# A hybrid decoder block: the state-space parameters' load, the pace of the state-space preparation, the transposes' banks and the place of the taps' matrices

## The chip, the cores and the metric

The kernel runs on one core of a Trainium2 chip. The metric is device time in microseconds (us), the median of three runs. Besides, one execution was recorded by the hardware profiler; the profile and the trace are of that one. Engines are named as in the profile: PE is TensorE, PEld its weight loads, DVE is VectorE, ACT is ScalarE, POOL is GpSimd, SP is SyncE. Each engine takes its own instructions in order and waits for others through semaphores.

## The reference

A decoder block over 528 positions (16 learned ones and 512 of the sequence), width 2048, float32. From one RMS-normalised input two branches are computed, latent attention with 16 heads and a diagonal complex state-space layer; both are gated, added, projected, and followed by a SwiGLU feed-forward part and a last norm.

```
n = rms_norm(h, norm_mix)
q_lat, kv_lat, k_r, u, gates = split(n @ w_in)
q, kv = rms_norm(q_lat) @ w_q_up, rms_norm(kv_lat) @ w_kv_up      # 16 heads
attn_out = mla_attention(q_nope, rope(q_rope), k_nope, rope(k_r), v) @ w_attn_proj
# state space: 64 groups, 64 states, 16 channels each
step = exp(log_step); ab = exp(lam * step); bb = (ab - 1) / lam * b
x[t] = ab * x[t-1] + bb @ u[t];  y[t] = Re(c @ x[t]) + d * u[t]
ssm_out = (gelu(y) @ w_glu_val) * sigmoid(gelu(y) @ w_glu_gate)
mixed = sigmoid(g0) * attn_out + sigmoid(g1) * ssm_out
h = h + mixed @ w_out
h = h + (silu(m @ w_ffn_gate) * (m @ w_ffn_up)) @ w_ffn_down,  m = rms_norm(h, norm_ffn)
out = rms_norm(h, norm_final)[16:]
```

## The kernel before

**Products.** Float32 products are made of three reduced ones: each operand is split into a high half (ACT rounds it, L262) and a low half (VectorE subtracts, L263), and TensorE adds high x high, high x low and low x high. Weights come as a stream of blocks of 128 x 1024 on SP's queue. `st.use()` hands out the next block and emits the splits of the blocks up to two ahead; the halves lie in rings of three.

**Order before the attention.** `dense` (L390) makes one output tile of 128 rows: sixteen weight tiles, two blocks, in banks of PSUM. PSUM has eight banks: psA and psB two each, psD two together, psQ and psV one each. The tiles are eight of u (the state-space input), four of q, four of kv, and one for the rotated key. u and kv tiles and the rope tile take psA and psB together, q tiles psA alone. When a tile is done VectorE evacuates it, for q and kv ACT squares it, and GpSimd or VectorE adds the squares.

**What runs beside.** After each block `dense` calls `bg()` (L364). It first runs what was put off to this turn (norms and pieces of norms), then it takes work from a generator. The generator says with each `yield` how much VectorE time it has just emitted, and each turn has an allowance of 5.0. Its work is emitted in program order into all engines, between the blocks. What is left after the rope tile is emitted at once by `run_out` (L935).

**The generator** is `ssm_first` (L663). `ssm_params` (L519) computes from 96 values a partition the powers of the discretised state matrix: exponentials, sine and cosine as polynomials on VectorE, then tables by doubling. Then, for each of four groups of 16 state-space groups:

- loads of b and d; copies on ACT into C48 (L709) and the first columns of the rotation table ER (L714), then two doublings of ER on VectorE (L717);
- `expand` twice (L724, L726), each of two halves of three VectorE products of 128 x 1024: the input matrix BL into ssA and the output matrix into ER;
- `taps` (L672): 64 small matmuls into psD, the response of the layer to one input over eight positions;
- `transposed` (L680): BL is turned by TensorE, four 128 x 128 transposes to a bank of psB, and evicted by ACT (L684) into BT, a tile in ssB; four such banks a group, then BT goes to DRAM;
- one group later `toeplitz` (L686): VectorE adds the direct term to the taps, eight DMAs store them (L690), GpSimd clears a tile of 128 x 2048 in ssB (L692), eight DMAs read the taps back shifted (L695), so that the tile holds a block-triangular matrix of taps for each of 16 state-space groups, and a DMA stores the tile (L697).

The matrices are read again only after the attention, by `load_t` in `ssm_main`. All these DMAs are issued by GpSimd, as are the stores of u (L874, eight a tile), the rope tables' load for the key (L938) and the DMA that moves half of the rotated key to other partitions (L943).

**The attention.** `run_out` is followed by the key's rope, then by a loop of turns, `for i in range(-1, HEADS + 1)`. In a turn the entries of `TURN` (L1173) are emitted for three heads: the scores of head i, transposes and value product of head i - 1, and key, query and value projections of head i + 1. GpSimd has in it: the loads of rotated queries `load_qs` into QS (L1005), a memset in every second turn (L1069), and after every fourth head two additions of `up_rope`, on which ACT then waits. The outputs of the heads are kept in `raw`, sixteen half tiles which lie in ssA, ssB, T1, T2, v and w; before, all are allocated ahead of the loop.

The sum of squares for a norm, `rstd_of` (L414), is made by a matmul with ones into psQ, and for 528 columns into psQ and psV.

Of the kernel before, what the change touches and what calls it, by code (L numbers as in the profile page):

```python
# [22 lines left out]
F32 = mybir.dt.float32  # L23
# [7 lines left out]
P = 128  # L31
# [3 lines left out]
SEQ = 512  # L35
# [11 lines left out]
CL = 8  # L47
NC_ = T // CL
BP = 8
BG = 16  # L50
# [247 lines left out]
def _emit(nc, sp, pp, dp, A, out):  # L298
# [3 lines left out]
    def sb(shape, dt, tag, bufs=1):  # L302
        cnt[0] += 1
        return sp.tile(shape, dt, tag=tag, name=f"{tag}_{cnt[0]}", bufs=bufs)
# [3 lines left out]
    def ps(shape, tag):  # L308
        cnt[0] += 1
        return pp.tile(shape, F32, tag=tag, name=f"ps{tag}_{cnt[0]}", bufs=BANKS[tag])  # L310
# [137 lines left out]
    POOL.dma_start(identb, A["identb"])  # L448
    mask = sb([P, P], BF, "mask")
    POOL.dma_start(mask, A["mask"])  # L450

    acc = sb([P, T], F32, "acc")
    rstd_x = sb([P, T], F32, "rstd")
# [63 lines left out]
             v(T1), v(T2))  # L517

    def ssm_params():  # L519
        prm = sb([P, 3, 32], F32, "sprm")  # L520
        POOL.dma_start(prm, A["sprm"])
        lr, li, ls = prm[:, 0], prm[:, 1], prm[:, 2]
        w = sb([P, 16, 32], F32, "sw")
        wi = sb([P, 32], I32, "swi")
# [16 lines left out]

        step, rr, th = w[:, 0], w[:, 1], w[:, 2:4]
        exp_(step, ls)
        yield 6
        tt(rr, lr, step, MUL)
        exp_(rr, rr)
        yield 6
        tt(w[:, 2], li, step, MUL)
        ts(w[:, 3], w[:, 2], 8.0, None, MUL)
        q, a, z = w[:, 4:6], w[:, 6:8], w[:, 8:10]  # L550
# [7 lines left out]
        ts(z, z, -MAGIC, None, ADD)  # L558
        stt(q, z, -4.0, q, MUL, ADD)
        tt(z, a, a, MUL)  # L560
        yield 3
        ts(sn, z, 1.0 / 362880, None, MUL)
        for c in (-1.0 / 5040, 1.0 / 120, -1.0 / 6):
            stt(sn, sn, c, z, ADD, MUL)
# [7 lines left out]
        ts(tA, tA, -1.0, 2.0, MUL, ADD)  # L572
        tt(q, q, tA, MUL)
        cs_, sn_ = w[:, 6:8], w[:, 2:4]
        yield 5
        tt(tA, sn, z, MUL)
        tt(sn_, co, q, MUL)
        tt(sn_, sn_, tA, ADD)
# [8 lines left out]
        tt(pw[:, 1, :, 1], rr, sn_[:, 0], MUL)  # L587
        t1 = w[:, 8:12].rearrange("p a b -> p (a b)")
        t2 = w[:, 12:16].rearrange("p a b -> p (a b)")
        yield 5  # L590
        for m in (1, 2, 4):
            bc = lambda i: pw[:, i, :, m:m + 1].to_broadcast([P, 32, m])
            v1 = t1[:, :32 * m].rearrange("p (a b) -> p a b", b=m)
# [3 lines left out]
        tt(e8[:, 2], rr, rr, MUL)  # L597
        tt(e8[:, 2], e8[:, 2], e8[:, 2], MUL)
        tt(e8[:, 2], e8[:, 2], e8[:, 2], MUL)
        yield 5  # L600
        nr, den, s1 = w[:, 8], w[:, 9], w[:, 10]
        ab_re, ab_im = pw[:, 0, :, 1], pw[:, 1, :, 1]
        ts(nr, ab_re, -1.0, None, ADD)
# [9 lines left out]
        tt(s1, nr, li, MUL)  # L613
        tt(cf[:, 1], cf[:, 1], s1, SUB)
        tt(cf[:, 1], cf[:, 1], den, MUL)
        yield 4

        T1 = sb([P, 2 * T], F32, "T1")
        T2 = sb([P, 2 * T], F32, "T2")
# [43 lines left out]
    def ssm_first():  # L663
# [14 lines left out]
            return pk  # L678

        def transposed(b, BL, BT, j):  # L680
            pt = ps([P, 4, P], "B")
            for i in range(4):
                PE.transpose(pt[:, i], BL[:, i % 2, j + i // 2], ident)
            ACT.activation(BT[:, j:j + 2].rearrange("p a b c -> p (a b) c"), pt, AF.Copy)  # L684

        def toeplitz(b, pk, Dg):  # L686
            g0 = b * BG
            tt(Dg, pk[:, :BG * 16], Dg, ADD)
            for i in range(CL):
                POOL.dma_start(kd[:, g0:g0 + BG, i], Dg[i * 16:(i + 1) * 16].rearrange("p (g o) -> p g o", o=16))  # L690
            TT = sb([P, BG, P], F32, "ssB")
            POOL.memset(TT, 0.0)  # L692
            for i in range(CL):
                s = CL - 1 - i
                POOL.dma_start(TT[i * 16:(i + 1) * 16, :, s * 16:],  # L695
                               kd[:, g0:g0 + BG, 0:i + 1].rearrange("p g t o -> p g (t o)"))
            POOL.dma_start(wt[b], TT.rearrange("p g m -> p (g m)"))  # L697

        behind = None
        for b in range(4):  # L700
# [17 lines left out]
                yield 1.0 + 0.05 * k  # L718
            POOL.dma_start(ed[b], ER.rearrange("p a j c -> p a (j c)"))
            if behind:  # L720
                toeplitz(*behind)
                yield 0.4
            BL = sb([P, 2, BP, CL * 16], F32, "ssA")
            yield from expand(BL, Bt, js, 0, 1, T1, T2)  # L724
# [11 lines left out]
            POOL.dma_start(bd[b], BT.rearrange("p j a c -> p (j a c)"))  # L736
            yield 0.1
        yield 5
        toeplitz(*behind)

    def ssm_main():

# [137 lines left out]
    for j in range(8):  # L880
        if j == 2:
            d2 = ps([P, 2, 512], "D")
            o = [(d2[:, 0, :HT], 0, HT), (d2[:, 1, :HT], HT, T)]
        else:
            o = halves("A", "B")
        dense(n, KT, o)
        pend.append((j, o))
        if j >= 2:
            while pend:
                evac_u(*pend.pop(0))  # L890
        if j == 2:
            beside(ssm_first(), 5.0)


    def normed(raw, acc_, nn, gcol, tag0, per):
# [48 lines left out]


    raw = {}
    for tag, h0, c in (("ssA", 0, 4), ("ssB", 4, 4), ("T1", 8, 2), ("T2", 10, 2), ("v", 12, 2), ("w", 14, 2)):
        t = sb([P, c, SEQ], F32, tag)
        for i in range(c):
            raw[h0 + i] = t[:, i]  # L950
    QS = sb([P, 2, SEQ], R, "U")
    pt01 = sb([P, 2, 4, P], R, "S10")
    pt23a = sb([P, 2, 4, P], R, "S11")
# [184 lines left out]
    def pv(h, pair):  # L1138
        if pair == 0:
            pvt[h] = ps([P, 512], "V")  # L1140
        o = pvt[h][:, pair * 256:(pair + 1) * 256]
        tm, ta = vt[h // 2]

        c = slice((h % 2) * P, (h % 2) * P + P)
        fl = lambda t, x, a: t[:, x, a:a + 2].rearrange("p a b -> p (a b)")
        mm(o, tm[:, c], ptm[:, 2 * pair:2 * pair + 2].rearrange("p a b -> p (a b)"), True, False)
        items = []
        srcs = [(1, pt01, 2), (2, pt01, 0)] if pair == 0 else \  # L1150
            [(1, pt23a, 0), (2, pt23a, 2), (3, pt23b, 2), (4, pt23b, 0)]
        for kb, t, a in srcs:
            v_ = ta[(kb - 1) // 2]
            items.append((v_[:, (kb - 1) % 2, 0, c], v_[:, (kb - 1) % 2, 1, c], fl(t, 0, a), fl(t, 1, a)))
        for n_, (vh, vl, ph, pl) in enumerate(items):
            mm(o, vh, ph, False, False)
            mm(o, vh, pl, False, False)
            mm(o, vl, ph, False, n_ == len(items) - 1)
        if pair == 1:
            ACT.activation(raw[h], pvt.pop(h), AF.Copy)  # L1160

    def rest():
# [32 lines left out]
    for i in range(-1, HEADS + 1):  # L1195
        norm_prev()
        for who, what in TURN:
            head = i + {"c": -1, "s": 0, "u": 1}[who]
            if 0 <= head < HEADS:
                what(head)  # L1200


    H2 = SEQ // 2
# [623 lines left out]
```

## Time and profile before

| | |
|---|---|
| median of three runs | 2838.66 us (2837.74 to 2839.67) |
| profiled execution | 2837.2 us, its span 2835.4 us |
| mean granted clock of TensorE | 0.986 |
| PE busy | 2747.7 us, 97% of the span |
| VectorE busy | 2049.9 us, 72% |
| ACT busy | 1222.6 us, 43% |
| GpSimd busy | 496.1 us, 17% |

Times in the trace are counted from the span's start. An instruction's row has its start, its length, engine, line of the kernel, operation, what it writes and reads, and in brackets how long the engine had stood idle before it and what ended that. DMA issues on GpSimd are shown with the time the engine took to issue them, not with the transfer. The granted clock is a share of full speed, and a mean under 1 in a stretch says that TensorE ran part of it slower. Blocks of DMA rows name the tile and its source (`ssB<-kd`: into a tile in ssB, from the taps in DRAM).

### The profile page before, as it was taken

To read this page: it belongs to the slowest core of one execution; us is meant where nothing else is said; L and a number is where in the kernel's file an instruction comes from. 1 tells how busy PE (TensorE), PEld (TensorE's weight loads), DVE (VectorE), ACT (ScalarE), POOL (GpSimd) and SP (SyncE) were. 2 spreads that over 40 slices of the span, in tenths; PEclk is the share of its full clock that TensorE was granted. 3 is DMA by queue.
4 is the path that set the end of the run, shared out by engine and by line. 5 is a ranking of instruction groups with operands and counts; after the bars stand their busy time and mean duration, and the time that the engine had idled before them with its cause. 6 is when DMAs were issued, how large, how long until landed. Compare 5 with 4: busy or idle time off the path is not lost.

```text
span 2835.4 us, 50272 instructions
## 1 busy us (share of the span) xinstructions
PE 2747.7 (97%) x20782; PEld 2593.5 (91%) x20782; DVE 2049.9 (72%) x2682; ACT 1222.6 (43%) x1786; POOL 496.1 (17%) x768
## 2 busy tenths in 40 slices
PE   8977899999999999999999999999999999999997
PEld 8867799977899999888889999999999999999997
DVE  6876566666367777433468888888888888788896
ACT  4223455542354445322234444444444445353445
POOL 3344211113221201112112000000000003030102
PEclk9988899999999999999999999999999999999998
DMA  5465222259664434444443343334333337474542
GB/s 173 127 193 159 92 68 68 68 201 352 213 231 158 164 138 160 142 148 139 135 135 135 135 139 127 137 127 142 128 126 134 135 133 255 164 268 164 198 160 97
DMA packets 129204, 436.86 MB, mean 154 GB/s; under 512 B 18736, under 2 KB 23536, under 8 KB 126864
## 3 DMA queue, kind: packets, MB, share of 16 engines
q1 hardware_dynamic: 76672, 263.36, 27.1%
q0 software_dynamic: 51520, 169.19, 18.0%
q8 instruction: 163, 2.67, 0.4%
q10 hardware_dynamic: 784, 1.11, 0.1%
q14 instruction: 65, 0.53, 0.1%
HBM read 348.61 MB, written 81.40 MB: 152 GB/s over the span
## 4 chain that ended last, share of the span: by engine, by line
PE 81%; DVE 6%; DMA 3%; issue 2%; POOL 1%; ACT 1%; DVEq 0%; ACTq 0%; POOLq 0%
PE psA L316 48%; PE psB L316 20%; PE psQ L316 6%; PE psV L316 5%; PE psD L316 1%; DVE wlo L263 1%; DVE S L323 1%; DVE T L323 1%; DVE ev L323 1%; DMA U<-ud 0%; DMA ER<-td 0%; PE psA L1127 0%; DMA ssB<-kd 0%; DMA T<-td 0%; DVE cmb L243 0%
## 5 line engine op out<-in xcount | busy, mean ns | idle before, releaser
L316 PE MATMUL psA<-S,whi 128*128 128x256 f32 (+2 forms) x5136 | 1124.1, 309 | 13.0 <-ACT whi L262 6.2
L316 PEld LDWEIGHTS psA<-S,whi 128*128 128x128 f32 x5136 | 845.6, 189 | 68.3 <-ACT whi L262 7.0
L316 PE MATMUL psA<-S,wlo 128*128 128x256 f32 (+2 forms) x2568 | 792.0, 308 | 8.9 <-DVE wlo L263 8.8
L263 DVE TENSOR_TENSOR wlo<-raw,whi 128x1024 fp32r<-128x1024 f32 (+1 forms) x479 | 591.8, 1236 | 184.6 <-ACT whi L262 182.5
L262 ACT ACTIVATE whi<-raw 128x1024 fp32r<-128x1024 f32 (+1 forms) x479 | 504.0, 1054 | 412.7 <-PE psA L316 182.5
L316 PEld LDWEIGHTS psA<-S,wlo 128*128 128x128 f32 x2568 | 485.5, 189 | 35.9 <-DVE wlo L263 10.4
L263 DVE TENSOR_TENSOR wlo<-cmb,whi 128x1024 fp32r<-128x1024 f32 x225 | 275.2, 1223 | 96.6 <-ACT whi L262 95.6
L316 PE MATMUL psB<-S,whi 128*128 128x256 f32 (+1 forms) x1632 | 331.2, 284 | 0.6 <-ACT ssB L684 0.5
L262 ACT ACTIVATE whi<-cmb 128x1024 fp32r<-128x1024 f32 x225 | 237.6, 1056 | 203.1 <-DVE wlo L263 138.9
L316 PEld LDWEIGHTS psB<-S,whi 128*128 128x128 f32 x1632 | 267.0, 191 | 1.4 <-ACT ssB L684 0.8
L316 PE MATMUL psB<-S,wlo 128*128 128x256 f32 (+1 forms) x816 | 231.0, 283 | 0.0
L316 PEld LDWEIGHTS psB<-S,wlo 128*128 128x128 f32 x816 | 155.0, 190 | 0.0
L1335 POOL DMA_DIRECT2D td<-sC x22 | 15.8, 717 | 764.6 <-ACT ev L1254 679.6
L316 PE MATMUL psA<-H,whi 128*128 128x512 f32 (+2 forms) x448 | 120.3, 356 | 15.1 <-DVE ev L323 11.3
L316 PEld LDWEIGHTS psA<-H,whi 128*128 128x128 f32 x448 | 78.1, 193 | 26.3 <-DVE ev L323 11.6
L243 DVE TENSOR_TENSOR cmb<-raw,raw 128x1024 f32<-128x1024 f32 x75 | 91.4, 1219 | 5.5 <-DMA raw<-in_wst 4.4
L323 DVE TENSOR_TENSOR H<-H,psA 128x256 f32<-128x256 f32 (+1 forms) x42 | 22.5, 536 | 97.2 <-POOL H L323 88.4
L243 DVE TENSOR_TENSOR cmb<-cmb,raw 128x1024 f32<-128x1024 f32 x75 | 91.5, 1220 | 0.0
L243 DVE TENSOR_TENSOR cmb<-raw,cmb 128x1024 f32<-128x1024 f32 x75 | 91.5, 1220 | 0.0
L243 DVE TENSOR_TENSOR raw<-raw,raw 128x1024 f32<-128x1024 f32 x75 | 91.4, 1219 | 0.0
L1254 ACT ACTIVATE ev<-psA 128x256 f32<-128x256 f32 x114 | 43.4, 381 | 100.6 <-PE psA L316 100.6
L316 PE MATMUL psA<-H,wlo 128*128 128x512 f32 (+2 forms) x224 | 78.2, 349 | 0.0
(680 smaller groups left out, 5464.7 us busy)
## 6 DMA issues: line engine op xcount, KB each, us to landing
raw<-in_wst SPq DMA_DIRECT2D x485, 512.0 KB, 3.7
td<-sC POOLq DMA_DIRECT2D x22, 512.0 KB, 3.2
td<-H POOLq DMA_DIRECT2D x40, 256.0 KB, 3.3
S<-td POOLq DMA_DIRECT2D x40, 256.0 KB, 6.9
H<-sg POOLq DMA_DIRECT2D x16, 512.0 KB, 3.9
cd<-ER POOLq DMA_DIRECT2D x8, 512.0 KB, 6.2
bd<-ssB POOLq DMA_DIRECT2D x4, 1024.0 KB, 4.8
wt<-ssB POOLq DMA_DIRECT2D x4, 1024.0 KB, 5.5
```

Source lines behind the costliest of these rows:

```text
L243: self.nc.vector.tensor_tensor(t, g(a), g(b), op=op)
L262: self.nc.scalar.activation(hi[:, a:b], w[:, a:b], AF.Copy)
L263: self.nc.vector.tensor_tensor(lo[:, a:b], w[:, a:b], hi[:, a:b], op=ALU.subtract)
L316: PE.matmul(o, lhsT=l, rhs=r, start=start, stop=stop, skip_group_check=more)
L323: eng.tensor_tensor(o, a, b, op=op)
L1254: ACT.activation(snap[name], o, AF.Copy)
L1335: POOL.dma_start(dst[0:2].rearrange("f p n -> p f n"), pair)
```

## The change

Five things are changed.

1. The 96 parameters a partition are loaded with the constants at the start, no longer at the generator's first step.
2. The amounts that `ssm_params` states with its yields are smaller, and the allowance of a turn is 4.7, no longer 5.0.
3. `transposed` writes into psQ and psV in turn, no longer into psB.
4. `toeplitz` is cut in two. In the generator `keep_taps` adds the direct term and stores the taps. The clearing, the shifted reads and the store are a new `toeplitz(b)` which the attention's loop calls at the end of its turns 0 to 4: turn i clears and reads the matrix of group i, in two tiles of half the size with eight reads each, and stores the two tiles of group i - 1. Groups 0 and 3 use ssB, group 1 T1 and T2, group 2 v and w.
5. The tiles of `raw` are allocated when the first head that lies in each is evicted.

```diff
@@ -448,6 +448,8 @@
     mask = sb([P, P], BF, "mask")
     POOL.dma_start(mask, A["mask"])
+    prm = sb([P, 3, 32], F32, "sprm")
+    POOL.dma_start(prm, A["sprm"])
@@ -517,8 +519,6 @@
     def ssm_params():
-        prm = sb([P, 3, 32], F32, "sprm")
-        POOL.dma_start(prm, A["sprm"])
...
         exp_(step, ls)
-        yield 6
+        yield 4.2
         tt(rr, lr, step, MUL)
         exp_(rr, rr)
-        yield 6
+        yield 4.4
...
-        yield 3
+        yield 2.4
...
-        yield 5
+        yield 3.6
...
-        yield 5
+        yield 2.4
...
-        yield 5
+        yield 4.4
...
-        yield 4
+        yield 3.2
@@ -678,23 +678,16 @@
         def transposed(b, BL, BT, j):
-            pt = ps([P, 4, P], "B")
+            pt = ps([P, 4, P], "QV"[j // 2 % 2])
...
-        def toeplitz(b, pk, Dg):
+        def keep_taps(b, pk, Dg):
             g0 = b * BG
             tt(Dg, pk[:, :BG * 16], Dg, ADD)
             for i in range(CL):
                 POOL.dma_start(kd[:, g0:g0 + BG, i], Dg[i * 16:(i + 1) * 16].rearrange("p (g o) -> p g o", o=16))
-            TT = sb([P, BG, P], F32, "ssB")
-            POOL.memset(TT, 0.0)
-            for i in range(CL):
-                s = CL - 1 - i
-                POOL.dma_start(TT[i * 16:(i + 1) * 16, :, s * 16:],
-                               kd[:, g0:g0 + BG, 0:i + 1].rearrange("p g t o -> p g (t o)"))
-            POOL.dma_start(wt[b], TT.rearrange("p g m -> p (g m)"))
...
             if behind:
-                toeplitz(*behind)
+                keep_taps(*behind)
                 yield 0.4
...
         yield 5
-        toeplitz(*behind)
+        keep_taps(*behind)
+
+    tt_parts = {}
+
+    def toeplitz(b):
+
+        if b:
+            for i, t in enumerate(tt_parts[b - 1]):
+                POOL.dma_start(wt[b - 1, :, i * 8 * P:(i + 1) * 8 * P], t.rearrange("p g m -> p (g m)"))
+        if b == 4:
+            return
+        if b in (1, 2):
+            tt_parts[b] = [sb([P, 8, P], F32, t) for t in (("T1", "T2"), ("v", "w"))[b - 1]]
+        else:
+            t = sb([P, BG, P], F32, "ssB")
+            tt_parts[b] = [t[:, :8], t[:, 8:]]
+        for h, t in enumerate(tt_parts[b]):
+            g0 = b * BG + h * 8
+            POOL.memset(t, 0.0)
+            for i in range(CL):
+                s = CL - 1 - i
+                POOL.dma_start(t[i * 16:(i + 1) * 16, :, s * 16:],
+                               kd[:, g0:g0 + 8, 0:i + 1].rearrange("p g t o -> p g (t o)"))
@@ -889,7 +904,7 @@
         if j == 2:
-            beside(ssm_first(), 5.0)
+            beside(ssm_first(), 4.7)
@@ -1157,6 +1169,10 @@
         if pair == 1:
+            if h in RAWS:
+                tag, c = RAWS[h]
+                t = sb([P, c, SEQ], F32, tag)
+                raw.update((h + i, t[:, i]) for i in range(c))
             ACT.activation(raw[h], pvt.pop(h), AF.Copy)
@@ -1198,6 +1214,8 @@
             if 0 <= head < HEADS:
                 what(head)
+        if 0 <= i < 5:
+            toeplitz(i)
```

More of the change, by code (lines that the diff above doesn't have):

```diff
@@ L946, in _emit @@
     raw = {}
[L947 to L950, printed above, removed]
+    RAWS = {0: ("ssA", 4), 4: ("ssB", 4), 8: ("T1", 2), 10: ("T2", 2), 12: ("v", 2), 14: ("w", 2)}
     QS = sb([P, 2, SEQ], R, "U")
```

## The prediction

> **What bounds the kernel now.** I read the page's forty slices first, then busy time and granted clock by stage, then TensorE's waits, and last the order of single instructions on VectorE, GpSimd, ScalarE and TensorE up to the attention. A slice is 70.9 us.
>
> ```profile
> span 2835.4 us, 50272 instructions
> ...
> PE   8977899999999999999999999999999999999997
> ...
> PEclk9988899999999999999999999999999999999998
> ```
>
> TensorE is full nearly everywhere but in slices 2 to 5, and there the granted clock is down too. In the next view each row is a stretch: its length, the busy time of PE, weight load, DVE, ACT and POOL, the clock, and DMA. The stretches are the last five u tiles, the q tiles, most of the kv tiles, the rope tile with what leads into the attention, and the attention.
>
> ```profile
> 47.50:108.00 60.50, 57.71 (x478) 57.39 (x477) 43.62 (x158) 9.58 (x10) 30.00 (x60) 1.00 0.47 120
> 108.00:189.00 81.00, 70.52 (x451) 59.59 (x451) 63.01 (x86) 22.06 (x46) 34.28 (x59) 0.92 0.58 172
> 189.00:246.00 57.00, 43.96 (x382) 41.79 (x382) 42.68 (x56) 12.34 (x23) 24.67 (x40) 0.85 0.57 157
> 246.00:301.00 55.00, 33.12 (x235) 29.64 (x232) 27.33 (x36) 15.25 (x31) 18.91 (x34) 0.75 0.49 146
> 301.00:580.00 279.00, 276.67 (x2040) 259.18 (x2040) 190.44 (x433) 155.17 (x371) 46.84 (x80) 1.00 0.23 68
> ```
>
> From 47.5 to 301 TensorE idles 48 us and loses clock besides; over the attention it idles 2 in 279. Ten blocks of eight weight tiles take 57.7 us, so a block is 5.8. The waits of TensorE in this stretch (total, times, longest):
>
> ```profile
> PE psB L683 <- ACT ssB L684: 17.0, 5, 10.4
> PE psA L316 <- DVE ev L323: 11.3, 1, 11.3
> PE psA L316 <- DVE wlo L263: 8.8, 4, 2.9
> PE psB L683 <- DVE H L323: 7.5, 1, 7.5
> ```
>
> The transposes of the tables wait for their evictions or for a psB bank, the blocks for the low half of the weights, and the first key tile for a bank that VectorE empties late. Behind nearly all of it stands VectorE, which takes its instructions in order: a low half is split two blocks ahead of its use, so TensorE waits for one only when VectorE is that far behind. So I cost the change on VectorE's order and carry the lead over to TensorE.
>
> **The parameters' load.**
>
> ```profile
> 61.03 0.58 POOL L521 DMA_DIRECT2D sprm<-in_sprm  x1
> ```
> ```profile
> 63.18 0.18 DVE L332 TENSOR_SCALAR sw<-sprm 128x32 f32<-128x32 f32 x1 [13.21 <-DMA sprm<-in_sprm]
> ```
>
> The load stands on GpSimd behind 24 stores of u, and VectorE stops 13.2 us for it. Issued with the constants it has landed long before; its one issue of 0.58 falls where GpSimd has nothing else, so I cost it at nothing (0.6 without that cover). VectorE's lead is 13.2. From below it is worth nothing to TensorE, if the lead only becomes waiting elsewhere; from above 13.2.
>
> **The smaller yields and the allowance of 4.7.** The yields sum to 130.8, spent in 27 turns of 5.0; now to 121.4, spent in 26 turns of 4.7. The arithmetic on VectorE is the same, so the sum has no term of its own. What moves is the place. The last expansion of the fourth group falls into kv tile 2's second block, no longer into kv tile 3's first. All four sets of transposes now come after the first block of a tile, in the middle of its accumulation, no longer at its end. That is one block earlier for each set, while the matmuls of that block still have to be done.
>
> **The transposes in psQ and psV, and ssB without the taps' matrix.** ACT's eviction of the fourth set waits 7.3 us for the store of the matrix that shares ssB; VectorE waits for the copies that stand behind such evictions on ACT.
>
> ```profile
> 256.30 1.23 ACT L684 ACTIVATE ssB<-psB 128x512 f32<-128x512 f32 x2 [7.33 <-DMA wt<-ssB]
> ```
> ```profile
> L684 ACT ACTIVATE ssB<-psB 128x512 f32<-128x512 f32 x4 | 2.4, 592 | 3.6 <-PE psB L683 3.6
> ...
> L709 ACT ACTIVATE U<-v 64x128 f32<-64x128 f32 x2 | 0.6, 302 | 0.0
> ```
> ```profile
> DVE T L323 <- ACT H L714: 16.1, 4, 6.8
> ```
>
> Once the matrix is out of ssB that wait has no cause. Two transposes at a time still need two evictions, and these still stand on ACT behind the square of the tile before and the high half of a weight. For each of the three later waits I take 3.7: four evictions (2.4) and eight copies of 0.3, overlapped to some 2.0, less 0.7 of VectorE's own work. The first stays at 0.8. Together 11.9 against 16.1: gain 4.2. Bounds: all gone, 16.1; three times the longest, 6.8 each, loss 5.
>
> psQ also holds the sum of squares of q, written just ahead of the third set, so that set waits for VectorE to read it. VectorE then is in its backlog, and ACT's eviction is bound by the same backlog; I add nothing (bounds 0 and 3).
>
> Where the first matmul after the fourth set now falls:
>
> ```profile
> 252.68 1.23 DVE L323 TENSOR_TENSOR ER<-T,T 128x1024 f32<-128x1024 f32 x1
> ...
> 254.96 0.42 DVE L323 TENSOR_TENSOR H<-psA,rstd 128x264 f32<-128x264 f32 x1
> ```
> ```profile
> 204.43 1.23 DVE L263 TENSOR_TENSOR wlo<-raw,whi 128x1024 fp32r<-128x1024 f32 x1 [1.66 <-ACT whi L262]
> ```
> ```profile
> 258.57 0.57 PE L316 MATMUL psA<-S,whi 128*128 128x264 f32 x1
> ```
> ```profile
> 265.54 0.61 PE L316 MATMUL psQ<-KS,ones 128*128 128x264 f32 x2
> ```
>
> The last expansion ended at 252.7 + 1.2 = 253.9. Now it ends 13.2 + 4.2 earlier, and one tile border earlier in the order: two evacuations (0.8), the idle 1.7 while ACT squares and makes the high half, and one low half (1.2) come after it, 3.7 in all. That is 253.9 - 21.1 = 232.8. After it: evacuation 0.8, ACT 1.7, and from ACT's first eviction to TensorE's next block 258.57 - 256.30 = 2.3. TensorE goes on at 237.6, 21.0 earlier than 258.6, but one block more (5.8) then lies ahead: 15.2. At 265.5 the sum of squares of kv is 15.2 earlier.
>
> **The matrices out of the way of the attention's start.**
>
> ```profile
> 275.61 1.83 POOL L692 MEMSET ssB<- 128x2048 f32 x1
> 277.73 4.39 POOL L695 DMA_DIRECT2D ssB<-kd  x8 [0.29 <-POOL ssB L692]
> 286.06 0.57 POOL L697 DMA_DIRECT2D wt<-ssB  x1 [3.94 <-DMA ssB<-kd]
> 286.62 0.55 POOL L938 DMA_DIRECT2D S<-in_kcs  x1
> ```
> ```profile
> 291.63 0.71 DVE L323 TENSOR_TENSOR S<-S 128x528 f32<-128x528 f32 x1 [10.53 <-DMA S<-in_kcs]
> ```
> ```profile
> 280.91 0.48 PE L316 MATMUL psA<-H,whi 128*128 128x264 f32 x2 [2.96 <-DVE S L323]
> ...
> 294.73 0.81 PE L316 MATMUL psA<-H,whi 128*128 128x264 f32 x2 [11.31 <-DVE ev L323]
> ```
>
> The rope table's load stands behind the fourth matrix, VectorE waits 10.5 for it, and the next key tile waits behind VectorE. Of the fourth matrix only the stores of the taps stay, a turn earlier; the table then lands while VectorE still norms kv. The 10.5 goes, and with the taps' addition 0.4 out of this chain: 10.9. Next late is VectorE's norm of kv (the 2.96 before 280.91), which stays. Bounds: 0, if another load takes its place, and 11.3. After the long gap two matmuls take 0.81 against 0.48 before it, the clock being halved; half speed up to about 298.5 costs some 1.9. A short gap may or may not halve it: I take 0.9.
>
> **What the attention gets in return.** Per turn, for the first four, two memsets of half the size, sixteen loads and, a turn later, two stores, all on GpSimd ahead of the next turn's loads of the rotated queries and of two rope additions.
>
> ```profile
> L695 POOL DMA_DIRECT2D ssB<-kd x32 | 17.5, 556 | 1.2 <-POOL ssB L692 1.2
> L692 POOL MEMSET ssB<- 128x2048 f32 x4 | 7.3, 1830 | 0.0
> ...
> L697 POOL DMA_DIRECT2D wt<-ssB x4 | 2.3, 586 | 21.7 <-DMA ssB<-kd 21.7
> ```
> ```profile
> 336.46 1.95 POOL L1005 DMA_DIRECT2D U<-ER  x4
> 358.19 1.29 POOL L323 TENSOR_TENSOR ev<-ev,ev 128x512 f32<-128x512 f32 x1 [19.78 <-DVE ev L323]
> ...
> 376.12 1.95 POOL L1005 DMA_DIRECT2D U<-ER  x4
> ```
> ```profile
> 364.58 0.63 ACT L319 ACTIVATE ER<-ev 128x512 fp32r<-128x512 f32 x1
> ```
> ```profile
> 394.61 0.66 PE psB L316 x6
> ```
>
> One matrix is 1.8 + 16 x 0.556 + 2 x 0.586 = 11.9 us of GpSimd. In the times of before, the second runs from 336.5 to 348.4, the queries' loads to 350.3, the third matrix to 362.2: the rope addition is 4.0 late, ending at 363.5, and ACT wants it at 364.6. The fourth runs from 376.1 to 388.0, the loads for head 5 end at 389.9, and its scores start at 394.6. Every delay fits, so I take 0; with no cover left, 4 us at each of four places, 16. Heads 0, 4, 8 to 14 take their output tiles only when they are evicted; the last store out of ssB is issued in the turn before head 4's eviction, which covers it. SP's queue is not passed by anything, and each load moves the bytes that it moved before, in two halves.
>
> L1005 is the quickest test of the issue's price while VectorE works on its normalisations:
>
> ```profile
> L1005 POOL DMA_DIRECT2D U<-ER x60 | 29.7, 505 | 51.6 <-PE psD L316 37.0 <-ACT S L319 13.6 <-ACT ER L319 0.9
> ```
> ```profile
> L330 DVE TENSOR_SCALAR S<-S,stats 128x240 f32<-128x240 f32 (+3 forms) x63 | 29.6, 469 | 4.9 <-DVE stats L1109 0.5
> ```
>
> The Trainium skill (SBUF — State Buffer, section "SBUF: two separate sides") speaks against the change: while VectorE runs an fp32 SBUF-to-SBUF operation in its two-port mode, GpSimd cannot write the descriptors of its DMAs, and an issue grows from about 620 to about 3100 ns. By that figure a matrix would be an estimated 58 us of GpSimd, four of them 232 against the 79 of four turns (two took 376.1 - 336.5 by the rows above), and the time about 2965. The 60 loads in this very stage took 505 ns, so the trace does not bear it out.
>
> **Sum.** 15.2 + 10.9 + 0.9 - 0 = 27.0. The profiled execution took 2837.2 (span 2835.4 and 1.8 around it), which gives 2810.2; the median of the runs, 2838.7, is 1.5 above it. Forecast: 2812.
>
> **The rivals.**
>
> *The lead passes whole.* If ACT frees the banks in time, the remaining 11.1 of waits before the doublings goes too: 38 saved, 2800. For it: TensorE's idle 48 us leave the room. Against it: the evictions stand behind VectorE's evacuation on ACT. 0.23.
>
> *The lead is eaten.* Sets in mid-tile wait for the tile before to be evacuated, the third also for psQ; the waits grow to 6.8 each (9 worse), and most of the 13.2 becomes TensorE's waiting. The rope table's 10.9 and 1 to 3 more remain: 2826. For it: the wait row of 16.1 shows VectorE already standing behind ACT. 0.19.
>
> *Slower: GpSimd's order in the attention.* If an issue takes 1.2 us there, one matrix is 23.4, the second and third in a row end 49 after 336.5, at 385, 20 after ACT wants the rope addition, and the fourth makes the queries of head 5 late by another 10. That is 30 against 27 gained: 2842 with the median. 1.2 is about the point from which it decides. Against it: the 505 and 556 above. 0.05.
>
> *It does little.* Fewer turns but no shorter path, the table's load still late behind the stores of the taps: 2837. 0.06.
>
> **How the numbers follow.** The forecast has 0.47. The range reaches from 2798, just past the first rival, to 2830, past the second; the bounds of the waits (16.1 to a loss of 5) lie within it. About 0.2% (5.7 us) is what a measurement here can tell from no change: faster 0.87, same 0.08, slower 0.05.
>
> **What would show it.** No wait of VectorE for sprm; none of ACT for the store out of ssB; none for the rope table; TensorE's idle time up to the attention near 30 instead of 48; waits before the doublings near 12; the granted clock still under 1 once or twice before the attention. In the attention, GpSimd busier, 505 to 560 ns an issue, and PE's idle time as before. A TensorE wait on QS or on the rope addition, or longer issues, would make the forecast wrong on the slow side; sets of transposes that follow their block at once, on the fast side.

## The result, and the profile after

The changed kernel takes 2796.81 us (median of four runs, 2794.86 to 2798.77); the kernel before took 2838.2 beside it (four runs, 2835.86 to 2839.67). The ratio is 0.9855 [0.9838, 0.9872]. 41.4 us are saved where 27 were forecast, and the time lies 1.2 below the forecast's range. The profiled execution of the changed kernel took 2798.77 us, with a span of 2796.8 and a mean granted clock of 0.989.

First the forty slices (69.9 us each now) of the changed kernel:

```profile
PE   9977999999999999999999999999999999999997
...
PEclk9988999999999999999999999999999999999999
```

The weak slices are fewer, but they lie where they lay. The stretches of the prediction, in the same columns (length; busy time and count of PE, weight load, DVE, ACT, POOL; clock; DMA):

```profile
47.50:108.00 60.50, 60.36 (x491) 59.77 (x491) 54.49 (x179) 13.28 (x19) 33.38 (x66) 1.00 0.52 138
108.00:189.00 81.00, 72.67 (x553) 61.86 (x551) 65.22 (x78) 18.94 (x37) 25.27 (x44) 0.98 0.52 159
189.00:246.00 57.00, 40.62 (x345) 39.80 (x346) 37.62 (x53) 17.01 (x31) 16.55 (x28) 0.79 0.47 134
246.00:301.00 55.00, 48.98 (x334) 45.13 (x333) 35.95 (x65) 26.17 (x59) 24.02 (x44) 0.94 0.43 120
301.00:580.00 279.00, 275.84 (x1961) 255.29 (x1959) 189.94 (x421) 155.71 (x365) 76.00 (x133) 0.99 0.30 91
```

The lengths less the busy times make TensorE's idle time from 47.5 to 301: 0.1 + 8.3 + 16.4 + 6.0 = 30.9, against 2.8 + 10.5 + 13.0 + 21.9 = 48.2 before. So 17.3 of idle time are gone. In the attention GpSimd is busy for 76.0 instead of 46.8, and TensorE idles 3.2 instead of 2.3.

To see where the rest was saved, both programs' matmuls were numbered from the end and the same ones compared. First four rows of the kernel before, then the same four matmuls of the kernel after: one at the start of the attention's turns, one late in them, one shortly before the feed-forward part, one late in that part.

```profile
322.49 0.23 PE L316 MATMUL psB<-mask,identb 128*128 128x128 bf16 x1
...
566.34 0.70 PE L316 MATMUL psA<-H,whi 128*128 128x512 f32 x2
...
1462.68 0.40 PE L316 MATMUL psA<-S,wlo 128*128 128x512 f32 x1
...
2278.74 0.40 PE L316 MATMUL psB<-ER,whi 128*128 128x256 f32 x2
```
```profile
296.57 0.23 PE L316 MATMUL psB<-mask,identb 128*128 128x128 bf16 x1
...
540.96 0.71 PE L316 MATMUL psA<-H,whi 128*128 128x512 f32 x2
...
1435.41 0.40 PE L316 MATMUL psA<-S,wlo 128*128 128x512 f32 x1
...
2243.76 0.39 PE L316 MATMUL psB<-ER,whi 128*128 128x256 f32 x2
```

The lead is 25.9, 25.4, 27.3 and 35.0; at the last matmul it is 2820.88 - 2782.52 = 38.4. (These are two single executions, and the changed kernel's is the slowest of its four; hence 38.4 and not 41.4.) So the part that the forecast worked out, up to the attention, came in at 25.9 against 27. The attention cost 0.5 against 0. Behind 1435 the changed kernel gains a further 11, and in that part of the code the change edits nothing. One view shows it as a rate. In these 340 us TensorE is busy from end to end at full clock in both kernels, first before, then after:

```profile
1900.00:2240.00 340.00, 340.00 (x2868) 340.00 (x2868) 281.42 (x297) 156.07 (x196) 14.51 (x24) 1.00 0.38 132
```
```profile
1900.00:2240.00 340.00, 340.00 (x2902) 339.55 (x2902) 284.74 (x301) 159.00 (x200) 14.51 (x24) 1.00 0.39 134
```

2868 matmuls in 340 us are one every 118.5 ns; 2902 are one every 117.2. Matmuls of the same part of the program, all of 256 columns and at the same clock, follow each other 1.4 ns sooner. No wait and no clock is in that view.

**What the change moved besides time: addresses.** A tile gets its place in SBUF when its name is first asked for. The tile of the parameters, 128 x 96 values of four bytes, is 384 bytes a partition. Before, it was asked for at the generator's first step, behind the tiles of the input (S0 to S15), the rings of the weights' halves, U and ev. Now it is asked for ahead of them. So all of these lie 384 bytes later, while the tiles that are asked for after the old place (T1, T2, v, w, ssA, ER, ssB, KS) stay where they were. The program's own allocation shows it, in bytes of a partition:

```
                  whi (first)  S1       S2       T1       T2       v        ssA      ER       ssB      KS
before              72800     97376   101600   176800   181024   185248   195744   203936   212384   224672
after               73184     97760   101984   176800   181024   185248   195744   203936   212384   224672
```

TensorE holds a half of the weights (whi or wlo) and streams one of the other tiles past it. I joined these addresses to the matmuls of the trace and grouped the 256-column ones between 1470 and 2750 us by the distance from the half's address to the streamed tile's, modulo 256 bytes (all the halves lie whole multiples of 4096 apart). Mean time from one matmul's start to the next's, in ns, without those that wait:

```
distance mod 256        0             64             128            192           all
before           118.0 (x2652)  118.0 (x3204)  119.3 (x3101)  116.7 (x666)      118.3
after            119.0 (x2722)  117.9 (x669)   117.2 (x3156)  114.0 (x3204)     116.7
```

The large group of T1, v, ssA, ssB, ER and KS went from a distance of 64 to one of 192, and its matmuls from 118.0 to 114.0. In exchange the small group of T2 and w went the other way. That isn't all of it. The S tiles moved together with the halves and kept their distances, and yet the group at 128 fell from 119.3 to 117.2 and the group at 0 rose from 118.0 to 119.0. By the counts the large group makes 12.8 us of the gain, the group at 128 another 6.6, and the group at 0 and that of T2 and w take 3.5 back. The distance of a matmul's own tile therefore can't be the whole account of the change's gain.

### The profile page after: what moved, and what is told of

It is laid out like the page before. It is cut to its first block, busy times and chain, and to the rows that moved or that the text cites. A ratio compares the mean times of both kernels' runs of the same rounds, so it can differ in the third digit from the quotient of the medians.

```text
span 2796.8 us, 50314 instructions
## 1 busy us (share of the span) xinstructions
PE 2727.5 (98%) x20782; PEld 2575.1 (92%) x20782; DVE 2046.9 (73%) x2682; ACT 1222.9 (44%) x1786; POOL 513.6 (18%) x808
## 4 chain that ended last, share of the span: by engine, by line
PE 87%; DVE 6%; DMA 2%; issue 2%; ACT 1%; POOL 1%; DVEq 0%; SPq 0%; ACTq 0%; POOLq 0%
PE psA L316 52%; PE psB L316 22%; PE psQ L316 6%; PE psV L316 5%; PE psD L316 1%; DVE T L323 1%; DVE wlo L263 1%; DVE ev L323 1%; DVE S L323 1%; ACT whi L262 1%; DVE H L323 0%; DMA ER<-td 0%; PE psA L1139 0%; DMA sw<-in_sb 0%; POOL T L753 0%
```

## The experiments

Two theories stood at the start. *Places*: the forecast is right for the edits as such, and the rest comes from the shift of 384 bytes. *Work*: something in the edits themselves (less traffic of DMAs, other banks) makes the feed-forward part quicker.

**Only the place.** The kernel before, with the parameters' tile asked for early and its load left where it was:

```diff
+    prm = sb([P, 3, 32], F32, "sprm")       # behind the mask's load
@@ def ssm_params():
-        prm = sb([P, 3, 32], F32, "sprm")
         POOL.dma_start(prm, A["sprm"])
```

> The kernel before, with nothing changed but the place of one tile: the parameters' tile of 384 bytes a partition is allocated with the constants, while its load stays where it was. So the weights' halves, S0 to S15, U and ev lie 384 bytes higher, and T1, T2, v, w, ssA, ssB, ER and KS stay. Theory 'addresses' (the 12.6 us that the changed kernel gains after 1460 us come from where the tiles lie): 12 to 13 us faster than before, about 2826, all of it after 1460 us; the first key tile that waited still starts near 294.7. Theory 'order' (those 12.6 us come from the changed order of the work ahead of the attention): no change, 2838.

2822.96 us, ratio 0.9948 [0.9936, 0.9961]: 15.0 saved (12 to 13 were expected), with no instruction added, removed or moved. The attention's row comes at 323.17, no earlier than before (322.49), and the late stretch has the rate of the changed kernel:

```profile
323.17 0.23 PE L316 MATMUL psB<-mask,identb 128*128 128x128 bf16 x1
```
```profile
1900.00:2240.00 340.00, 340.00 (x2901) 339.50 (x2900) 284.62 (x303) 158.90 (x200) 16.33 (x27) 1.00 0.39 132
```

By distance its matmuls take 119.0, 117.9, 117.3 and 113.9 ns, as in the changed kernel.

**The change without the shift.** The changed kernel, with all names asked for once, in the old order, ahead of everything that uses them:

```diff
+    for tag, n_, dt, bufs in ([("acc", T, F32, 1), ("rstd", T, F32, 1), ("S0", 2 * T, R, 1), ("whi", 1024, R, 3),
+                               ("wlo", 1024, R, 3)] + [(f"S{k}", 2 * T, R, 1) for k in range(1, 16)]
+                              + [("U", T, F32, 1), ("se8", 96, F32, 1), ("spw", 576, F32, 1), ("scf", 64, F32, 1),
+                                 ("ev", T, F32, 3)]):
+        for _ in range(bufs):
+            sb([P, n_], dt, tag, bufs)
     prm = sb([P, 3, 32], F32, "sprm")
```

> The changed kernel with the tiles put back to the addresses of before: the tags are allocated in the old order ahead of the parameters' tile, and nothing else is different. Theory 'addresses': about 12.5 us slower than the changed kernel, near 2810, which is the forecast's 2812; the gain at the attention's start stays at 25 to 26. Theory 'order': 2797 as the changed kernel.

2814.4 us (2808.98 to 2815.33), ratio 0.9912 [0.9898, 0.9925]. The attention's row comes at 296.75, the changed kernel's within 0.2; the late stretch has the old rate:

```profile
296.75 0.23 PE L316 MATMUL psB<-mask,identb 128*128 128x128 bf16 x1
```
```profile
1900.00:2240.00 340.00, 340.00 (x2867) 340.00 (x2867) 283.89 (x302) 155.39 (x195) 16.33 (x27) 1.00 0.38 134
```

So the five edits without their side effect save 23.5 us, and the forecast of 2812, which has no term for that effect, lies 2.4 from this kernel. The side effect is worth 15.0 by the one run and 2814.4 - 2796.8 = 17.6 by the other. *Work* falls as the cause of the late gain: all five edits are in this kernel, and its late rate is the old one.

**The edits one by one.** Three kernels at the old addresses tell the terms of the sum apart. Items 4 and 5 alone (the matrices in the attention, banks and load as before):

```diff
-                toeplitz(*behind)
+                keep_taps(*behind)
...
+        if 0 <= i < 5:
+            toeplitz(i)
```

> The kernel before with the matrices alone moved into the attention's turns; old yields, psB for the transposes, late load of the parameters, old addresses. By the forecast's terms: the rope table's 10.9, 4.2 for the copies behind ACT, 0.9 of clock: 16 us, 2822. Rival 'VectorE holds the rest': only the 10.9, 2827. Rival 'GpSimd's order in the attention': over 2838, with TensorE waiting for QS or for the rope addition.

Item 1 alone (the load early, with the old addresses held as in the run above):

```diff
+    prm = sb([P, 3, 32], F32, "sprm")
+    POOL.dma_start(prm, A["sprm"])
@@ def ssm_params():
-        prm = sb([P, 3, 32], F32, "sprm")
-        POOL.dma_start(prm, A["sprm"])
```

> The kernel before with the parameters loaded with the constants, at the old addresses, nothing else. By the forecast VectorE's lead of 13.2 passes: 2825, no wait for sprm, the sum of squares of kv 13 us earlier than 265.5. Rival 'the lead is eaten': 3 to 6 us at most, 2833, the 13.2 turning up as longer waits for the stores out of ssB and for psB.

And both together, with the old yields, the old allowance and psB, so that only items 2 and 3 are missing:

> The kernel before with the matrices moved and the parameters loaded early, both at the old addresses; old yields and allowance, transposes in psB. It lacks only the new pace and the transposes' banks of the changed kernel at the old addresses (2814.4). Theory 'the pace and the banks bring nothing': 2812 to 2816, the sum of squares of kv near 250. Rival 'they bring the lead through': 2820 or more, since the sets at a tile's end then wait for psB.

The end of VectorE's last expansion of the generator, the starts of two matmuls, all in us, and the time:

```
                          last expansion  sum of squares  start of   time     ratio
                               ends           of kv       the turns
before                         253.9          265.5         322.5    (2838)
matrices moved (4, 5)          249.0          256.6         302.6    2819.05  0.9930 [0.9915, 0.9946]
load early (1)                 246.4          258.0         315.0    2831.09  0.9975 [0.9964, 0.9985]
both (1, 4, 5)                 241.2          249.8         295.8    2811.43  0.9900 [0.9883, 0.9916]
all at the old addresses       233.9          251.6         296.8    2814.40  0.9912 [0.9898, 0.9925]
after                          233.7          250.7         296.6    2796.81  0.9855 [0.9838, 0.9872]
```

By the forecast's terms 16.0 were due from the matrices (4.2, in which the banks have a part, 10.9 and 0.9) and 13.2 from the load; beside 2837.93 for the kernel before, the runs saved 18.9 and 6.8. The second is nearer to the rival in which the lead is eaten (3 to 6) than to 13.2. The waits of VectorE from 45 to 312 us show what each of the two took away. The kernel before:

```profile
DVE wlo L263 <- ACT whi L262: 17.7, 10, 5.3
```

Matrices moved:

```profile
DVE wlo L263 <- ACT whi L262: 14.8, 11, 1.7
DVE sw L332 <- DMA sprm<-in_sprm: 13.5, 1, 13.5
DVE T L323 <- ACT H L707: 10.3, 4, 6.9
```

Load early:

```profile
DVE wlo L263 <- ACT whi L262: 22.7, 13, 5.2
DVE T L323 <- ACT H L720: 15.4, 4, 6.8
DVE S L323 <- DMA S<-in_kcs: 10.7, 1, 10.7
```

With the matrices moved the wait for the rope table is gone and the one for sprm stays; with the load early it is the other way round. The wait before the doublings goes down with the matrices (16.1 to 10.3), hardly with the load (15.4). With the load early VectorE waits 5.0 longer for high halves (17.7 to 22.7): a part of its lead runs into ACT. Items 2 and 3 together bring nothing that can be told: at the same addresses the turns start 0.9 earlier without them, and the two intervals overlap.

**What decides the rate.** Now the theory was *distance*: 192 bytes modulo 256 is quick. First, with the halves back at their old address, the streamed tiles were moved: 64 bytes ahead of S1, and 64 more ahead of the generator's tiles, which brings T1, v, ssA, ssB, ER, KS and the even S tiles from 64 and 128 to 192.

```diff
-                               ("wlo", 1024, R, 3)] + [(f"S{k}", 2 * T, R, 1) for k in range(1, 16)]
+                               ("wlo", 1024, R, 3), ("padS", 16, F32, 1)]
+                              + [(f"S{k}", 2 * T, R, 1) for k in range(1, 16)]
...
-                                 ("ev", T, F32, 3)]):
+                                 ("ev", T, F32, 3), ("sprm", 96, F32, 1), ("padT", 16, F32, 1)]):
```

> The changed kernel in the old order of tiles, with two unused pads of 64 bytes a partition, ahead of S1 and ahead of sw. Measured from the weights' halves, modulo 256 bytes, T1, v, ssA, ssB, ER and KS then lie at 192 as in the changed kernel, though the halves themselves are at other addresses; S2 to S15 lie at 192 and 64 by turns, no longer at 128 and 0. Theory 'the distance between weights and moving tile decides': 3 to 5 ns less per matmul on the even S tiles, about 1 on the odd ones, some 15 to 18 us in all; 2780. Rival 'the absolute address of the halves decides': 2808 to 2815, as with the old addresses.

2786.46 us, ratio 0.9811 [0.9796, 0.9826]: 10.4 under the changed kernel, where 15 to 18 were expected, and far from the rival's 2808 to 2815. Then the rest followed: within their tiles the operands of the odd S, of T2 and w start 128 bytes later, those of S0 64 bytes later, so that every one is at 192.

```diff
+    SHIFT = {"S0": 16, "T2": 32, "w": 32, **{f"S{k}": 32 for k in range(1, 16, 2)}}
+    def shifted(tag):
+        c = SHIFT.get(tag, 0)
+        if not c:
+            return sb([P, 2, SEQ], R, tag)
+        return sb([P, 2 * SEQ + c], R, tag)[:, c:].rearrange("p (a n) -> p a n", a=2)
```

> As the kernel with two pads, and the operands in S1, S3 to S15, T2 and w start 128 bytes into their tiles (64 in S0), so that all moving tiles from the second half of the kernel on lie at 192 from the weights' halves. By the distance: the mean of 116.8 ns of a 256-column matmul falls to about 114, over some 13,300 of them 30 to 38 us, 2760 to 2767. Rival 'the absolute address decides': 2808 to 2815. Rival 'not every pair gains': between 2770 and 2790.

2768.92 us (2766.13 to 2775.85), ratio 0.9753 [0.9737, 0.9768]: 69 to 71 us under the kernel before and 28 under the changed one. That is just outside the expected 2760 to 2767, and below the 2770 to 2790 of the rival in which not every pair gains. The late stretch, first with the two pads, then with all at 192:

```profile
1900.00:2240.00 340.00, 340.00 (x2915) 339.10 (x2915) 285.32 (x302) 159.06 (x200) 14.53 (x24) 1.00 0.39 134
```
```profile
1900.00:2240.00 340.00, 339.53 (x2975) 337.76 (x2975) 294.04 (x313) 161.57 (x202) 16.34 (x27) 1.00 0.41 140
```

116.6 ns, then 114.3. These two runs moved only streamed tiles; the change itself moved the halves, together with the S tiles, away from the others. To tell the distance from either address, the kernel with all at 192 was changed in two ways. In one, everything lies 64 bytes later, so that all addresses change and no distance does:

```diff
+    sb([P, 16], F32, "pad0")
     gv = sb([P, 56], F32, "gv")
```

> The kernel with all operands aligned (2768.92), with a pad of 64 bytes ahead of every other tile, so that all tiles lie 64 bytes later and every distance between a moving tile and a weights' half stays as it was. Theory (the distance alone decides): the same time, 2766 to 2776, and 256-column matmuls still every 114 to 115 ns, so some 2970 matmuls between 1900 and 2240 us as there (2975). Rival (the address of the moving tile or of the halves decides, taken for itself): matmuls go back to 116 to 119 ns, 2860 to 2920 in those 340 us, and the time to 2785 to 2815.

In the other, the pad ahead of S1 goes ahead of the halves: the halves alone lie 64 bytes later, and all distances become 128:

```diff
-     ("S0", 2 * T, R, 1), ("whi", 1024, R, 3), ("wlo", 1024, R, 3), ("padS", 16, F32, 1)]
+     ("S0", 2 * T, R, 1), ("padS", 16, F32, 1), ("whi", 1024, R, 3), ("wlo", 1024, R, 3)]
```

> The kernel with all operands aligned (2768.92), with the one pad of 64 bytes moved from ahead of S1 to ahead of the rings of weights' halves: only the halves lie 64 bytes later, every moving tile stays where it was, and all distances become 128 modulo 256 where they were 192. Theory (distance): 128 took 117.2 to 118.8 ns a matmul, so about 2870 to 2900 matmuls between 1900 and 2240 us instead of 2975, and the time goes back to 2800 to 2820. Rival (the moving tile's own address decides): the same time as before this edit, 2766 to 2776.

With everything later 2770.82 us (2768.15 to 2781.24), ratio 0.9776 [0.9756, 0.9796], as fast as before this edit. With the halves later 2818.57 (2815.76 to 2820.21), ratio 0.9935 [0.9919, 0.9952]: one pad of 64 bytes in another place costs 49.7 us. The late stretch of each, in that order:

```profile
1900.00:2240.00 340.00, 339.74 (x2932) 338.63 (x2931) 287.87 (x305) 160.48 (x203) 16.33 (x27) 1.00 0.38 134
```
```profile
1900.00:2240.00 340.00, 340.00 (x2860) 340.00 (x2859) 283.14 (x302) 155.25 (x195) 16.32 (x27) 1.00 0.38 134
```

The halves' shift gave 118.9 ns where 117.2 to 118.8 were expected. The common shift kept the time but not quite the count: 2932 where some 2970 were expected. Over 1470 to 2750 the matmuls by distance give the cleaner answer (most of the few at another distance have weights that are kept in other tiles, near the end):

```
distance mod 256        0             64             128            192           all
all at 192       119.3 (x294)   117.6 (x40)    118.3 (x81)    114.4 (x9509)     114.6
all 64 later     119.2 (x279)   117.7 (x40)    118.2 (x74)    114.3 (x9549)     114.5
halves 64 later  116.7 (x8)     117.7 (x20)    118.9 (x9602)  119.4 (x37)       118.9
```

The missing 38 matmuls are a matter of when. Both quick kernels have stretches at a slower pace, but not at the same times: here 2120 to 2160 and 2400 to 2440, first of the one with all at 192, then of the one with all 64 later.

```profile
2120.00:2160.00 40.00, 39.95 (x353) 39.75 (x351) 35.37 (x39) 18.92 (x24) 1.81 (x3) 1.00 0.42 142
2400.00:2440.00 40.00, 40.00 (x342) 40.00 (x341) 31.83 (x37) 15.29 (x15) 2.86 (x4) 1.00 0.45 160
```
```profile
2120.00:2160.00 40.00, 40.00 (x341) 39.96 (x341) 33.21 (x37) 18.31 (x23) 2.67 (x5) 1.00 0.42 151
2400.00:2440.00 40.00, 40.00 (x356) 40.00 (x355) 32.72 (x38) 15.84 (x15) 2.86 (x4) 1.00 0.48 167
```

353 or 356 matmuls in the quick ones, about 113 ns each; 342 or 341 in the slow ones, 117. The distance is the same in all four. The kernel before shows the same of a mixed layout: its matmuls at 128 whose next one streams a tile at 0 took 113.9 ns (x219) from 800 to 1090 us and 118.4 (x928) from 1470 to 2750, while in the changed kernel they took 114.0 and 114.3, at the same distances.

So with all tiles at one distance, 192 allows the quick pace and 128 doesn't, and the absolute address isn't what decides between these two. Whether a stretch takes the quick pace is decided by something else as well, and what that is stays open. So does how the 15 to 18 us of the change divide between the distance and that: only a shift of everything by 64 bytes, with all at 192, was run, and none by 384 from the old layout.

## Why the prediction was right and wrong

**The step that failed** is the sum's last one: 27.0 is taken off the profiled time as if all behind the start of the attention, but for the turns that it costs at 0, took as long as before. The prediction never says so and gives it no bounds. The parameters' tile is costed only as a load that is issued earlier; that item 1 also moves the place at which the tile is asked for, and so shifts S0 to S15, the halves' rings, U and ev by 384 bytes, has no term. The runs put that at 15.0 and 17.6 us of the 41, enough to leave the range; with the old addresses held, 2814.4 lies inside it. The diff shows it, since the line that asks for the tile moves with the load; what it would be worth no row quoted there could have told.

**VectorE's lead at the sum of squares of kv.** Forecast 15.2; the matmul went from 265.5 to 250.7, 14.8. The path was as forecast. In the changed kernel VectorE's last expansion and what follows it, and TensorE's next block:

```profile
232.44 1.23 DVE L323 TENSOR_TENSOR ER<-T,T 128x1024 f32<-128x1024 f32 x1
233.59 0.43 DVE L323 TENSOR_TENSOR H<-psA,rstd 128x264 f32<-128x264 f32 x1
...
236.07 1.48 DVE L263 TENSOR_TENSOR wlo<-raw,whi 128x1024 fp32r<-128x1024 f32 x1 [1.72 <-ACT whi L262]
```
```profile
238.19 0.57 PE L316 MATMUL psA<-S,whi 128*128 128x264 f32 x1
```

The expansion ends at 233.7 (forecast 232.8), the evacuations, the idle time and the low half come behind it, and TensorE goes on at 238.2 (forecast 237.6). The block more costs 5.5 (5.8 forecast): from there to the sum of squares it is 12.5, and was 7.0.

The sizes of the terms on VectorE were not right. By the first column of the table above, the load alone brings the expansion 7.5 forward, where the sum took it at 13.2; 5.0 of the 13.2 came back as VectorE's waits for high halves, by the rows above. Moving the matrices brings it 4.9 forward (4.2 in the sum). The new places, with the banks, bring it from 241.2 to 233.9, 7.3, where the sum took 3.7. One term too large by 5.7 and one too small by 3.6 nearly cancel: the near hit of 15.2 is partly luck. On TensorE the new places give nothing in the end: without items 2 and 3 the lead at the sum of squares is 15.7. With ssB free of the matrix, more than the store's wait went: TensorE's wait of 7.5 for a psB bank behind H is 0.6 in the run with the matrices moved.

**The waits before the doublings.** Forecast 11.9, from 16.1. The waits of VectorE up to the attention, after:

```profile
DVE wlo L263 <- ACT whi L262: 17.6, 13, 2.6
DVE T L323 <- ACT H L707: 11.2, 4, 4.1
```

11.2, with the longest at 4.1 where 3.7 was taken: right. None is left for sprm and none for the rope table, as forecast. The waits for high halves, 17.7 before, are 17.6 in all. Those for the load of b grew from 0.7 to 2.4.

**The banks.** TensorE's waits, after:

```profile
PE psQ L683 <- ACT ssB L684: 17.9, 4, 9.1
PE psQ L683 <- DVE ev L332: 4.3, 1, 4.3
PE psA L316 <- DVE S L323: 2.6, 1, 2.6
PE psA L316 <- DVE ev L323: 2.4, 1, 2.4
```

The transposes wait for ACT as long as before (17.9 and 17.0), at psQ now instead of psB: other banks didn't shorten it, since ACT's evictions are what it waits for. The third set does wait for the sum of squares of q in psQ, 4.3, above the bounds of 0 and 3. As the prediction said, it stands mostly inside the backlog: with psB kept, the turns start only 0.9 earlier.

**The matrices off the attention's start.** Forecast 10.9 and 0.9 for the clock. From the sum of squares of kv to the turns it was 322.49 - 265.54 = 56.95 and is now:

```profile
250.70 0.69 PE L316 MATMUL psQ<-KS,ones 128*128 128x264 f32 x2
```
```profile
250.56 0.58 POOL L953 DMA_DIRECT2D S<-in_kcs  x1
```
```profile
266.04 0.71 DVE L323 TENSOR_TENSOR S<-S 128x528 f32<-128x528 f32 x1
```

296.57 - 250.70 = 45.87, so 11.1 against 11.8. The rope table's load is issued at 250.56 and VectorE's multiplication by it at 266.04 waits for nothing; the wait of 2.96 behind the norm stays as 2.6. The gap of 11.31 is 2.4.

**The clock** is inside these leads, and larger than its term. By the stretches' clocks, TensorE ran (1 - 0.92) x 81 x 2 + 0.15 x 57 x 2 + 0.25 x 55 x 2 = 58 us at half speed before, and 0.02 x 81 x 2 + 0.21 x 57 x 2 + 0.06 x 55 x 2 = 34 after. Of the 25.9 gained, 17.3 are idle time, and the other 8.6 can only be busy time that became shorter; 24 us less at half speed allow for 12. The forecast's idle of 30 was met at 30.9. The prediction names both a lead of 27 and some 18 of idle time that goes, and gives only 0.9 of clock between them; the rows show why the two differ by more: waits that go take their half-speed matmuls with them.

**The attention.** Forecast 0, found 0.5 (243.85 us from row to row before, 244.39 after). GpSimd's rows there:

```profile
L1017 POOL DMA_DIRECT2D U<-ER x53 | 26.5, 513 | 30.6 <-PE psD L316 20.4 <-ACT S L319 9.1 <-ACT ER L319 1.1
L753 POOL DMA_DIRECT2D T<-kd x16 | 8.5, 541 | 0.6 <-POOL T L750 0.6
L753 POOL DMA_DIRECT2D ssB<-kd x16 | 8.4, 531 | 0.6 <-POOL ssB L750 0.6
```

531 to 541 ns an issue: the forecast's price of 505 to 556 holds, and the rival on the slow side falls with it. Of the 108 issues from 296 to 542 us only 20 overlap a TENSOR_SCALAR of VectorE, as its normalisations are, by more than 0.2 us; these took 552 ns on the mean and 722 at the most. The Trainium skill's figure of about 3100 ns (SBUF — State Buffer, section "SBUF: two separate sides") is that of a DMA beside VectorE's `tensor_copy`; for the operations of this stage it isn't borne out by the moved issues either.

**The rivals.** The lead passes whole (2800) is nearest in time and wrong in its reason: the waits before the doublings stayed at 11.2. The lead is eaten, and it does little, fall with the 25.9.

## What to carry to other kernels

When an edit moves the line that asks for a tile, it moves the tiles between the old place and the new one; compare the addresses of the two programs before putting a gain or a loss down to the work that was moved. A stage that the edit doesn't touch is the control: count matmuls there in a stretch without waits, and if the rate differs, hold the places fixed and measure again. In a kernel that TensorE bounds, the distance between the weights' tile and the streamed tile is worth a try by itself: here, for matmuls of 256 columns, it gave 45.5 us (2814.4 to 2768.9), the five edits 23.5.

## What the runs showed of the hardware that was not expected

**The spacing of matmuls depends on where their operands lie to each other.** With 128 x 128 weights and 256 columns in the reduced format, it was 113 to 114 ns in the quick stretches with all distances at 192 bytes modulo 256, and 118.9 with all at 128. From the layout with all at 192, everything moved together by 64 bytes changed nothing that the time shows; the halves moved alone by 64 bytes cost 49.7 us. Matmuls of 512 columns, from 1120 to 1440 us, show none of this: 233.4 ns at 192, in the one layout, and 233.1 at 128, in the other. The Trainium skill (TensorE: Matmul & The Clock Gate, section "Wait — 56ns, not 53.3ns?") gives N over 2.4 GHz and some 2.5 ns more for the step from matmul to matmul, by which 256 columns would be an estimated 109 ns at any address; that page doesn't have these addresses in it, and no stretch here reached it. Why 192, whether the read of the next weights meets that of the streamed tile, whether 256 is the right modulus, and why distance 192 took 116.7 in the kernel before, for T2 and w, stay open: no run here tells.

**A gap of 2.40 us was once enough to halve the clock.** In the kernel before, TensorE stood for 2.40 us, and then the spacing of its 512-column matmuls nearly doubled:

```profile
124.40 0.40 PE L316 MATMUL psA<-S,wlo 128*128 128x512 f32 x1
124.63 0.62 PE L316 MATMUL psA<-S,whi 128*128 128x512 f32 x2
127.65 0.63 PE L316 MATMUL psA<-S,wlo 128*128 128x512 f32 x1 [2.40 <-DVE wlo L263]
128.07 1.06 PE L316 MATMUL psA<-S,whi 128*128 128x512 f32 x2
```
```profile
127.60:131.10 3.50, 3.45 (x9) 2.71 (x10) 3.47 (x4) 0.00 (x0) 0.00 (x0) 0.54 0.51 147
131.10:135.00 3.90, 3.90 (x33) 3.02 (x31) 2.25 (x4) 2.53 (x3) 0.00 (x0) 0.98 0.02 6
```

The half speed lasted 3.4 us, and the pieces in both kernels, but for the last of each, at the program's end, are whole multiples of that: 3.4, 6.8, 10.2, 13.7 and 17.1. The Trainium skill (TensorE: Matmul & The Clock Gate, section "What's actually happening") has a free-running window of 3.4 us; the lengths agree with it. Its rule that a gap should stay under some 3.4 us (section "HAM oscillation — how this bites in real kernels") is too wide for this kernel, where 2.40 was enough.

The length of the gap alone doesn't tell. A longer one, 60 us earlier in the same kernel, left the clock as it was:

```profile
67.78 0.39 PE L316 MATMUL psA<-S,wlo 128*128 128x264 f32 x1 [2.79 <-DVE wlo L263]
68.00 0.28 PE L316 MATMUL psB<-S,wlo 128*128 128x264 f32 x1
```

In the trace's record of the clock the drops at 127.87, 158.59 and 250.75 lie whole multiples of 3.413 apart. Counted back in such steps, the 2.40 lie within one step (124.46 to 127.87), while an edge at 66.43 cuts the 2.79 into two pieces of 1.4. So it seems to be the idle part of one such step that counts; that is inferred from these rows and was not tested.
